# Eight dense tokens moved from the first expert pass to row gathers, in a one-core PEER layer

## The chip, the cores and the metric

The kernel runs on one core of one Trainium2 chip. The metric is the device time of one execution in microseconds. One execution was also profiled, and the rows below come from its trace. TensorE (PE) does the matmuls, VectorE (DVE), ScalarE (ACT) and GpSimd (POOL) the elementwise work, and SyncE (SP) issues most loads; indirect row gathers are issued by POOL.

## The reference, cut to what matters

One layer on 512 tokens of width 1024. A gated token mixer comes first, then PEER: each token picks, in each of 8 heads, 16 of 128 x 128 = 16384 single-neuron experts, so 128 experts a token.

```python
def peer(xn, w_q, sub_keys, u_tab, v_tab):
    ...
    s_top, i_top = lax.top_k(sc, PEER_TOPK)                    # two half-key scores per head
    ...
    best, pos = lax.top_k(cand..., PEER_TOPK)                  # 16 of 256 candidates
    idx = ...; g = softmax(best)
    ue = u_tab[ib]; act = gelu(einsum("phkd,pd->phk", ue, tb)) # first table: 128 rows a token
    ve = v_tab[ib]
    return einsum("phk,phkd->pd", gb * act, ve)                # second table: 128 rows a token
```

The output is RMSNorm(x + mixer + PEER), float32, 512 x 1024.

## The kernel before

Tokens lie in four tiles of 128. Tile 0 is served by **gathers**: for each of its 128 expert slots one indirect DMA brings 128 rows of 4 KB (one expert row for each token), first from `u_tab` (`ru`; a DVE multiply with the normed tokens `t0`, summed into a column of `d0`), later from `v_tab` (`rv`; DVE adds the row, times its weight, to `acc0`). That is 256 gathers.

Tiles 1 to 3, 384 tokens (`TD`), are **dense**: they go against both whole tables, 128 blocks of 128 experts each. A block of the first table is 24 matmuls into `ph` (8 slices of the width, 3 products each of a high and a low part), with 128 expert columns as weights and 384 token columns moving; ACT takes the gelu (`hg`). 62 of these blocks are done early, as filling between other work, and 56 of those results are put into DRAM (`hd`) and read back (`hr`). The other 66 are done in the last loop. A block of the second table is 18 matmuls into `acc` (6 for each token tile), with 128 tokens of `wh`/`wl` as weights and 512 columns of the table moving.

The stages in order: input projections and mixer (to 345 us), output projection and second norm (`turn`, L332 to L341), the query stage (16 steps: projection `pq`, scores `pc`, top-16 on DVE), the gate stage, and the last loop (L838). In the gate stage three rounds of 8 steps turn indices and gates into dense gate tiles: each step makes two `one_hot` groups of 8 tokens on DVE, 32 short matmuls into `pg` and copies to `stg`; between the rounds `stg` is written to DRAM (`gd`) while 7 more `ph` blocks run. Every third step issues a gather. In the last loop, iteration i loads a `v_tab` block, splits it into `hi` and `lo` (ACT, DVE), makes `wf`, `wh`, `wl` from gates and `hg`, runs the 18 matmuls, then one `ph` block while there is one, then releases `pace[i]` gathers: ACT copies the indices (`eix`), POOL issues, DVE consumes; up to `GLEFT` gathers stay unconsumed in program order. `pace` shares the gathers out by weights: 2 while `ph` blocks remain (66 iterations), `GTAIL` in the next 58, 0 in the last 4. The rows of gathers lie in two rings used in turn, of `GR` = 3 and `DR` buffers. `hi`/`lo` have 3 buffers, shared by both tables; `raw` has 7.

The query stage and the gate stage keep the written order on each engine; elsewhere a scheduler may move instructions.

Of the kernel before, what the change touches and what calls it, by code (L numbers as in the profile page):

```python
# [8 lines left out]
F32 = mybir.dt.float32  # L9
# [8 lines left out]
P = 128  # L18
# [9 lines left out]
TG = TD - P  # L28
EPS = 1e-6
# [21 lines left out]
DR = 5  # L51
GTAIL = 0.5
LATE = 3
FP = (1, 2)
GLEFT = 5
GR = 3
TWO = ("xa", "xc", "cv", "hh", "yb", "gga", "sma")
# [3 lines left out]
def tile_block(ctx: ExitStack, tc: tile.TileContext, x, w_in, vecs, w_ax, w_out, n2row, w_q, skT,  # L61
# [21 lines left out]
    x2d = dram.tile([NTT, P, D], F32, name="x2d")  # L83

# [70 lines left out]
    with ExitStack() as fctx:  # L155
# [193 lines left out]
    d0 = gp.tile([P, P], F32, name="d0")  # L349

# [6 lines left out]
    def gather(tab, n, name):  # L357
        ix = gidx.get(name, ei0[:, n:n + 1])
# [35 lines left out]
    def h_mm(i, hi, lo):  # L394
        pt = ps_a(f"ph{i}")
        mm3(pt[:, :TD], lambda k: hi[:, k * P:(k + 1) * P], lambda k: lo[:, k * P:(k + 1) * P],
            lambda k: a1h[:, k, P:], lambda k: a1l[:, k, P:], range(KD))
        return pt

    def h_act(i, pt):  # L400
        g = ha.tile([P, TD], F32, tag="hg", name=f"hg{i}", bufs=AHEAD)
        act.activation(g, pt[:, :TD], AF.Gelu_apprx_tanh)
        if i >= NKEY - SPILL:
            act.dma_start(hd[i - (NKEY - SPILL)], g)
        else:
            hg[i] = g

    def h_get(i):
        if i not in hg:
            hg[i] = ha.tile([P, TD], F32, tag="hg", name=f"hr{i}", bufs=AHEAD)  # L410
            sync.dma_start(hg[i], hd[i - (NKEY - SPILL)])
        return hg[i]

    hd = dram.tile([max(SPILL, 1), P, TD], F32, name="hd")
# [43 lines left out]
    with ExitStack() as qctx:  # L458
# [197 lines left out]
    def gather_release(n, i):  # L656
        names, p = [], gpos[0]
        while len(names) < n and p < len(gsched):
            f, a = gsched[p]
            if f is not gather_w:  # L660
                names.append(("ru" if f is gather_u else "rv") + str(a))
            p += 1
        if names:
            t = dp.tile([P, 4], I32, tag="eix", name=f"eix{i}", bufs=4)
            for m, nm in enumerate(names):
                c = int(nm[2:])
                tc.keep_in_program_order(act.activation(t[:, m:m + 1], eall[:, 0, c:c + 1], AF.Copy))  # L667
# [13 lines left out]
    with ExitStack() as gctx:  # L681
# [22 lines left out]
        dve.scalar_tensor_tensor(g12[:, :, 1, :], by_sub(ptg), GSC, g12[:, :, 0, :], op0=ALU.mult, op1=ALU.subtract)  # L704

# [44 lines left out]
        NSUB = NDT * P // OC  # L750
        ohs = {u: one_hot(u) for u in range(OB)}
        h_turn(HPRO2, dve)
        for t_ in range(NDT):
            stg = sp.tile([P, P, P], F32, tag="stg", name=f"stg{t_}", bufs=1)
            for s2 in range(P // OC // 2):
                sub = t_ * (P // OC) + 2 * s2

                def mid():
                    for u in (sub, sub + 1):
                        gate_mm(u, *ohs.pop(u))  # L760
# [8 lines left out]
                gather_steps(GSTEP[(sub // 2) % len(GSTEP)], 2)  # L769
# [21 lines left out]
    gdone = sum(1 for f, _ in gsched[:gpos[0]] if f is not gather_w)  # L791
    ng = 2 * P - gdone
# [41 lines left out]

    late = []
    vr = {}
    fgb = None
    for i in range(NKEY):  # L838
# [4 lines left out]
        wf = dp.tile([P, TD], F32, tag="wf", name=f"wf{i}", bufs=2)  # L843
# [4 lines left out]
        dve.tensor_tensor(wf[:, TG:], stg[:, i, :], hv_[:, TG:], op=ALU.mult)  # L848
# [71 lines left out]
```

## Time and profile before

| | |
|---|---|
| median of 3 runs | 1619.81 us (1617.53 to 1622.06) |
| the profiled execution | 1617.53 us, of which the span in the trace is 1615.4 us |
| PE busy, weight load busy | 1595.6 us (99%), 1412.5 us (87%) |
| DVE, ACT, POOL busy | 1264.4 us (78%), 688.2 us (43%), 510.8 us (32%) |
| granted TensorE clock, mean | 0.999 of full speed |
| bytes moved | 379.09 MB, 235 GB/s over the span |

Busy times are unions over the span. A matmul's duration in the trace holds its fill and drain, so that matmuls in a row overlap, and the time that one costs is the distance from start to start.

### The profile page before, as it was taken

The page shows a single profiled execution, that of the slowest core. Times are in us where ns is not written, and L with a number is a line of the kernel's source. Part 1 is how long each engine was busy: PE and PEld are TensorE (multiplying, and loading weights), DVE is VectorE, ACT ScalarE, POOL GpSimd, SP SyncE. Part 2 cuts the span into 40 slices and gives each one's busy share as a digit, 9 for nine tenths or more (in the row PEclk, how much of TensorE's full clock was granted, in tenths as well). Part 3 has the DMA queues.
Part 4 walks back from the last instruction along what each step waited for, and adds up shares of the span by engine and source line. Part 5 has one row for each costly group of instructions (what it writes and reads, how often), then busy time and mean ns, then how long its engine had stood idle before and what let it go on. Part 6 is the DMA issues. An engine that isn't in the chain of part 4 may idle for free.

```text
span 1615.4 us, 23573 instructions
## 1 busy us (share of the span) xinstructions
PE 1595.6 (99%) x8402; PEld 1412.5 (87%) x8402; DVE 1264.4 (78%) x2404; ACT 688.2 (43%) x1222; POOL 510.8 (32%) x379
## 2 busy tenths in 40 slices
PE   9999999999999999999999999999999999999997
PEld 8888888888988999999999888989998988887886
DVE  6666666645999997676878888888888789877767
ACT  7444444434333454454533433344333343333334
POOL 0000000004787840000045554545444554223231
PEclk9999999999999999999999999999999999999999
DMA  6222222334333356969499999999999999998884
GB/s 243 95 95 95 95 95 95 91 112 175 107 124 112 126 180 189 304 214 301 153 317 328 344 324 331 342 328 332 340 335 336 323 334 362 340 320 288 305 305 153
DMA packets 158453, 379.09 MB, mean 235 GB/s; under 512 B 14080, under 2 KB 78592, under 8 KB 158208
## 3 DMA queue, kind: packets, MB, share of 16 engines
q1 hardware_dynamic: 112832, 230.25, 41.6%
q0 software_dynamic: 36864, 134.23, 23.5%
q10 hardware_dynamic: 8640, 13.11, 2.3%
q8 instruction: 65, 1.06, 0.3%
q14 instruction: 52, 0.43, 0.1%
HBM read 345.56 MB, written 31.98 MB: 234 GB/s over the span
## 4 chain that ended last, share of the span: by engine, by line
PE 70%; DVE 9%; DMA 8%; issue 7%; POOL 3%; ACT 1%; SPq 1%; DVEq 0%; POOLq 0%; ACTq 0%
PE ph L147 7%; PE ph L149 7%; PE ph L148 7%; PE acc L830 7%; PE acc L833 6%; PE acc L829 6%; PE pin L149 6%; PE pin L147 6%; PE pin L148 6%; DMA ru<-in_u_tab_dram,eix 4%; DMA rv<-in_v_tab_dram,eix 3%; POOL rv L362 2%; PE pq L147 2%; PE pq L149 2%; PE pq L148 2%
## 5 line engine op out<-in xcount | busy, mean ns | idle before, releaser
L147 PE MATMUL ph<-a1h,hi_u 128*128 128x384 f32 x1024 | 346.3, 338 | 0.0
L149 PE MATMUL ph<-a1h,lo_u 128*128 128x384 f32 x1024 | 343.6, 336 | 0.6 <-POOL lo_u L108 0.4
L148 PE MATMUL ph<-a1l,hi_u 128*128 128x384 f32 x1024 | 342.7, 335 | 0.0
L830 PE MATMUL acc<-lo_v,wh 128*128 128x512 f32 x768 | 301.0, 392 | 5.1 <-DVE lo_v L108 5.1
L829 PE MATMUL acc<-hi_v,wh 128*128 128x512 f32 x768 | 299.5, 390 | 0.0
L362 POOL DMA_INDIRECT rv<-in_v_tab_dram,eix x128 | 168.1, 1313 | 265.0 <-ACT eix L667 229.7
L833 PE MATMUL acc<-hi_v,wl 128*128 128x512 f32 x768 | 238.7, 390 | 0.0
L362 POOL DMA_INDIRECT ru<-in_u_tab_dram,eix x120 | 161.0, 1341 | 216.7 <-ACT eix L667 178.3
L385 DVE SCALAR_TENSOR_TENSOR acc<-rv,w,acc 128x1024 f32<-128x1024 f32 x128 | 164.4, 1285 | 75.8 <-DMA rv<-in_v_tab_dram,eix 75.4
L107 ACT ACTIVATE hi_v<-raw_v 128x1024 fp32r<-128x1024 f32 x128 | 135.0, 1055 | 182.8 <-PE ph L148 169.3
L371 DVE SCALAR_TENSOR_TENSOR ru<-ru,t 128x1024 f32<-128x1024 f32 x128 | 155.7, 1222 | 57.0 <-DMA ru<-in_u_tab_dram,eix 56.9
L148 PEld LDWEIGHTS ph<-a1l,hi_u 128*128 128x128 f32 x1024 | 192.3, 188 | 2.6
L147 PEld LDWEIGHTS ph<-a1h,hi_u 128*128 128x128 f32 x1024 | 192.3, 188 | 2.6
L149 PEld LDWEIGHTS ph<-a1h,lo_u 128*128 128x128 f32 x1024 | 192.1, 188 | 1.5 <-POOL lo_u L108 0.8
L849 ACT ACTIVATE wh<-wf 128x384 fp32r<-128x384 f32 x128 | 67.0, 524 | 268.9 <-PE acc L830 193.0
L830 PEld LDWEIGHTS acc<-lo_v,wh 128*128 128x128 f32 x768 | 144.2, 188 | 38.9 <-DVE lo_v L108 10.1
L149 PE MATMUL pin<-a1h,lo_in 128*128 128x512 f32 x448 | 174.4, 389 | 0.3 <-POOL lo_in L108 0.3
L148 PE MATMUL pin<-a1l,hi_in 128*128 128x512 f32 x448 | 174.4, 389 | 0.0
L147 PE MATMUL pin<-a1h,hi_in 128*128 128x512 f32 x448 | 174.3, 389 | 0.0
L833 PEld LDWEIGHTS acc<-hi_v,wl 128*128 128x128 f32 x768 | 144.1, 188 | 30.7
L829 PEld LDWEIGHTS acc<-hi_v,wh 128*128 128x128 f32 x768 | 144.1, 188 | 27.4 <-ACT hi_v L107 0.2
L108 DVE TENSOR_TENSOR lo_v<-raw_v,hi_v 128x1024 fp32r<-128x1024 f32 x128 | 155.9, 1218 | 3.4 <-ACT hi_v L107 3.4
(199 smaller groups left out, 2469.9 us busy)
## 6 DMA issues: line engine op xcount, KB each, us to landing
raw_u<-in_uT_dram SPq DMA_DIRECT2D x128, 512.0 KB, 5.4
raw_v<-in_v_tab_dram SPq DMA_DIRECT2D x128, 512.0 KB, 5.6
raw_in<-in_w_in_dram SPq DMA_DIRECT2D x56, 512.0 KB, 3.3
gd<-stg SPq DMA_DIRECT2D x8, 2048.0 KB, 17.8
gt<-gd SPq DMA_DIRECT2D x128, 128.0 KB, 5.0
hd<-hg ACTq DMA_DIRECT2D x56, 192.0 KB, 3.4
hr<-hd SPq DMA_DIRECT2D x56, 192.0 KB, 5.5
raw_q<-in_w_q_dram SPq DMA_DIRECT2D x16, 512.0 KB, 3.2
```

Of the source, the lines that this page charges most:

```text
L107: act.activation(hi, raw, AF.Copy)
L108: lo_eng.tensor_tensor(lo, raw, hi, op=ALU.subtract)
L147: pe.matmul(pt, wh(k), xh(k), start=start and m == 0, stop=False)
L148: pe.matmul(pt, wh(k), xl(k), start=False, stop=False)
L149: pe.matmul(pt, wl(k), xh(k), start=False, stop=stop and m == n - 1)
L362: ins = pool.indirect_dma_start(out=rows, out_offset=None, in_=tab, in_offset=bass.IndirectOffsetOnAxis(ap=ix, axis=0))
L371: dq.append(lambda: dve.scalar_tensor_tensor(rows, rows, 1.0, t0, op0=ALU.mult, op1=ALU.mult, accum_out=d0[:, n:n + 1]))
L385: dq.append(lambda: dve.scalar_tensor_tensor(acc0, rows, w0[:, n:n + 1], acc0, op0=ALU.mult, op1=ALU.add))
L829: pe.matmul(accs[t][h], wh[:, ts], hi[:, hsl], start=first, stop=False)
L830: pe.matmul(accs[t][h], wh[:, ts], lo[:, hsl], start=False, stop=False)
L833: pe.matmul(accs[t][h], wl[:, ts], hi[:, hsl], start=False, stop=last)
L849: act.activation(wh, wf, AF.Copy)
```

## The change

The last eight tokens of tile 3 (`TE` = 8) leave the first pass: `ph` and `hg` become 376 columns wide (`TDE`), and the gate stage makes 47 groups of eight tokens instead of 48. These eight tokens have 8 x 128 = 1024 expert rows in each table. They are gathered with 16 partitions to a token, so that 8 gathers of 128 rows bring the `u_tab` rows (`xxu`) and 8 the `v_tab` rows (`xxv`). For this the normed rows `tx` are made on POOL, written to DRAM and read back with each row on 16 partitions (`te`); indices and gates take the same way (`ee`, `eg`). DVE sums the weighted `v_tab` rows in `acce`, and in iteration 48 (`XADD`) a one-hot matmul adds the 16 partitions of each token into `acc` of tile 3. The second pass keeps its width: the eight columns of `wf` are zero. `DR` goes from 5 to 4, `GLEFT` from 5 to 4, `GTAIL` from 0.5 to 0.7, and the gate stage issues no gather in its first two steps.

```diff
+TE = 8
+TDE = TD - TE
-DR = 5
-GTAIL = 0.5
+DR = 4
+GTAIL = 0.7
-GLEFT = 5
+GLEFT = 4
+XADD = 48
...
+        tx = fp.tile([P, D], F32, tag="junk", name="tx", bufs=1)
+        pool.tensor_scalar(tx, xs[NTT - 1], r, None, op0=ALU.mult)
+        pool.tensor_tensor(tx, tx, n2b, op=ALU.mult)
         turn_out(pts, 12, a1h, a1l)
...
+        act.dma_start(txd, tx[P - TE:, :])
...
+    def gather_xu(n):
+        rows = gather(u_tab, n, f"xxu{n}")
+        dq.append(lambda: dve.scalar_tensor_tensor(rows, rows, 1.0, te, op0=ALU.mult, op1=ALU.mult,
+                                                   accum_out=de[:, n:n + 1]))
+
+    def gather_xw(_):
+        act.activation(de, de, AF.Gelu_apprx_tanh)
+        dve.tensor_tensor(de, de, eg, op=ALU.mult)
+
+    def gather_xv(n):
+        rows = gather(v_tab, n, f"xxv{n}")
+        def add():
+            if n == 0:
+                acce.append(gp.tile([P, D], F32, tag="te", name="acce", bufs=1))
+                dve.tensor_scalar(acce[0], rows, de[:, 0:1], None, op0=ALU.mult)
+            else:
+                dve.scalar_tensor_tensor(acce[0], rows, de[:, n:n + 1], acce[0], op0=ALU.mult, op1=ALU.add)
+        dq.append(add)
...
-        mm3(pt[:, :TD], lambda k: hi[:, k * P:(k + 1) * P], lambda k: lo[:, k * P:(k + 1) * P],
-            lambda k: a1h[:, k, P:], lambda k: a1l[:, k, P:], range(KD))
+        mm3(pt[:, :TDE], lambda k: hi[:, k * P:(k + 1) * P], lambda k: lo[:, k * P:(k + 1) * P],
+            lambda k: a1h[:, k, P:P + TDE], lambda k: a1l[:, k, P:P + TDE], range(KD))
...
+            if s_ == 8:
+                for e in range(TE):
+                    sync.dma_start(te[e * EK:(e + 1) * EK, :], txd[e:e + 1, :].partition_broadcast(EK))
...
-    gsched = []
+    gsched = [(gather_xu, n) for n in range(TE)]
     for h in range(HEADS):
         for n in range(h * TOPK, (h + 1) * TOPK):
             gsched.append((gather_u, n))
+        if h == 0:
+            gsched.append((gather_xw, 0))
+            gsched.extend((gather_xv, n) for n in range(TE))
...
+        last = (NTT - 1, slice(P - TE, P))
+        act.dma_start(eed, eall[last[1], last[0], :])
+        act.dma_start(egd, gall[last[1], last[0], :])
+        for e_, d_ in ((ee, eed), (eg, egd)):
+            pool.dma_start(e_, d_.rearrange("e (k n) -> (e k) n", n=TE))
...
-        NSUB = NDT * P // OC
+        NSUB = TDE // OC
...
-                gather_steps(GSTEP[(sub // 2) % len(GSTEP)], 2)
+                if sub // 2 == 1:
+                    act.activation(eei, ee, AF.Copy)
+                if sub // 2 > 1:
+                    gather_steps(GSTEP[(sub // 2) % len(GSTEP)], 2)
...
+    wfs = [dp.tile([P, TD], F32, name=f"wf{m}") for m in range(2)]
+    for wf in wfs:
+        dve.memset(wf[:, TDE:], 0.0)
...
-        dve.tensor_tensor(wf[:, TG:], stg[:, i, :], hv_[:, TG:], op=ALU.mult)
+        dve.tensor_tensor(wf[:, TG:TDE], stg[:, i, :P - TE], hv_[:, TG:], op=ALU.mult)
...
+        if i == XADD:
+            bf = dp.tile([P, TG], F32, tag="gt", name="bf", bufs=4)
+            br = strm.tile([P, TD], F32R, tag="wh", name="br", bufs=3)
+            dve.memset(bf[:, :P], 0.0)
+            dve.tensor_reduce(bf[:, P - TE:P], ident.rearrange("p (e k) -> p e k", k=EK), op=ALU.add, axis=AX.X)
+            act.activation(br[:, :P], bf[:, :P], AF.Copy, scale=GSC)
+            hi, lo = split(acce[0], "acce", dve)
+            for part in (hi, lo):
+                for h in range(2):
+                    pe.matmul(accs[NDT - 1][h], br[:, :P], part[:, h * 512:(h + 1) * 512], start=False, stop=False)
```

## Rows read from the trace of the kernel before

**Rows 1.** The page: busy time by engine; shares of the chain that ended last.

```profile
PE 1595.6 (99%) x8402; PEld 1412.5 (87%) x8402; DVE 1264.4 (78%) x2404; ACT 688.2 (43%) x1222; POOL 510.8 (32%) x379
...
PE 70%; DVE 9%; DMA 8%; issue 7%; POOL 3%; ACT 1%; SPq 1%; DVEq 0%; POOLq 0%; ACTq 0%
```

**Rows 2.** Windows: stretch and length; busy time (instructions) by engine; clock, DMA share, GB/s.

```profile
395.00:515.00 120.00, 120.00 (x631) 107.44 (x630) 115.84 (x625) 41.00 (x75) 94.97 (x75) 1.00 0.36 121
515.00:565.00 50.00, 50.00 (x281) 47.90 (x280) 49.52 (x255) 18.23 (x38) 41.04 (x28) 1.00 0.35 120
565.00:665.00 100.00, 98.75 (x760) 96.81 (x759) 78.20 (x66) 47.89 (x76) 20.67 (x10) 1.00 0.66 207
...
740.00:795.00 55.00, 52.72 (x470) 50.93 (x469) 50.16 (x50) 29.45 (x51) 1.68 (x1) 1.00 0.60 205
795.00:1353.00 558.00, 554.32 (x2794) 502.12 (x2793) 465.67 (x649) 217.78 (x481) 263.25 (x201) 1.00 0.93 329
1353.00:1594.00 241.00, 239.81 (x1054) 197.23 (x1053) 189.93 (x307) 92.79 (x167) 65.83 (x47) 1.00 0.89 312
```

**Rows 3.** Windows of tile ph alone: PE busy, weight loads busy, ACT busy.

```profile
395.00:515.00 120.00, 45.63 (x249) 42.76 (x250) 4.92 (x10) 1.00 0.36 121
...
565.00:665.00 100.00, 83.17 (x466) 79.88 (x465) 9.78 (x20) 1.00 0.66 207
...
795.00:1353.00 558.00, 289.66 (x1598) 280.01 (x1596) 31.69 (x67) 1.00 0.93 329
```

**Rows 4.** Timeline of PE, first and last of 18 matmuls 384 wide (start, duration).

```profile
902.02 0.33 PE L147 MATMUL ph<-a1h,hi_u 128*128 128x384 f32 x1
...
904.97 0.33 PE L149 MATMUL ph<-a1h,lo_u 128*128 128x384 f32 x1
```

**Rows 5.** Timeline of PE, first and last of 19 matmuls 512 wide.

```profile
99.76 0.39 PE L149 MATMUL pin<-a1h,lo_in 128*128 128x512 f32 x1
...
103.84 0.39 PE L149 MATMUL pin<-a1h,lo_in 128*128 128x512 f32 x1
```

**Rows 6.** Timeline of PE: eight matmuls 128 wide with four-byte weights, and the next.

```profile
393.44 1.06 PE L515 MATMUL pc<-sks,qs 128*128 128x128 f32 x8
394.25 0.48 PE L147 MATMUL pq<-a1h,hi_q 128*128 128x512 f32 x1
```

**Rows 7.** Chain that ended last, gate stage: start, length, what.

```profile
729.01 19.74 DMA gd<-stg
...
785.42 1.15 DVE oij L714
786.59 1.24 DVE o L716
```

**Rows 8.** Timeline of POOL where the query stage begins.

```profile
382.55 0.18 POOL L461 IOTA ic<- 128x50 f16 x1 [366.75 <-PE pt_n L133]
382.71 2.41 POOL L108 TENSOR_TENSOR lo_q<-raw_q,hi_q 128x1024 fp32r<-128x1024 f32 x1
```

**Rows 9.** Groups by line: gathers and their consumers (busy, mean ns; idle before).

```profile
L362 POOL DMA_INDIRECT rv<-in_v_tab_dram,eix x128 | 168.1, 1313 | 265.0 <-ACT eix L667 229.7 <-issue 15.5 <-DVE acc L385 7.2
L385 DVE SCALAR_TENSOR_TENSOR acc<-rv,w,acc 128x1024 f32<-128x1024 f32 x128 | 164.4, 1285 | 75.8 <-DMA rv<-in_v_tab_dram,eix 75.4
...
L371 DVE SCALAR_TENSOR_TENSOR ru<-ru,t 128x1024 f32<-128x1024 f32 x128 | 155.7, 1222 | 57.0 <-DMA ru<-in_u_tab_dram,eix 56.9
```

**Rows 10.** Waits: who waited for whom, us in total, times, longest.

```profile
DVE acc L385 <- DMA rv<-in_v_tab_dram,eix: 75.4, 44, 5.0
...
ACT stg L729 <- DMA gd<-stg: 6.7, 1, 6.7
...
PE acc L830 <- DVE lo_v L108: 5.1, 9, 1.0
```

**Rows 11.** DMA issues: queue, count, size, median us to landing.

```profile
raw_v<-in_v_tab_dram SPq DMA_DIRECT2D x128, 512.0 KB, 5.6
raw_in<-in_w_in_dram SPq DMA_DIRECT2D x56, 512.0 KB, 3.3
```

More of the change, by code (lines that the diff above doesn't have):

```diff
@@ L83, in tile_block @@
     x2d = dram.tile([NTT, P, D], F32, name="x2d")
+    txd = dram.tile([TE, D], F32, name="txd")
+    eed = dram.tile([TE, P], F32, name="eed")
+    egd = dram.tile([TE, P], F32, name="egd")
+    EK = P // TE
     @contextmanager
@@ L349, in tile_block @@
     d0 = gp.tile([P, P], F32, name="d0")
+    ee = gp.tile([P, TE], F32, name="ee")
+    eg = gp.tile([P, TE], F32, name="eg")
+    eei = gp.tile([P, TE], I32, name="eei")
+    de = gp.tile([P, TE], F32, name="de")
+    te = gp.tile([P, D], F32, tag="te", name="te", bufs=1)
     ha = ctx.enter_context(tc.tile_pool(name="ha", bufs=1))
@@ L357, in gather @@
     def gather(tab, n, name):
-        ix = gidx.get(name, ei0[:, n:n + 1])
+        ix = gidx[name] if name in gidx else (eei if name[1] == "x" else ei0)[:, n:n + 1]
         rp, nb = rpool[gcnt[0] % len(rpool)]
@@ L372, in gather_u @@
                                                    accum_out=d0[:, n:n + 1]))
+    def gather_xu(n):
[5 more added lines that the diff above has]
+        dve.tensor_tensor(de, de, eg, op=ALU.mult)
+    acce = []
+    def gather_xv(n):
[7 more added lines that the diff above has]
+        dq.append(add)
     def drain(left):
@@ L395, in h_mm @@
         pt = ps_a(f"ph{i}")
-        mm3(pt[:, :TD], lambda k: hi[:, k * P:(k + 1) * P], lambda k: lo[:, k * P:(k + 1) * P],
-            lambda k: a1h[:, k, P:], lambda k: a1l[:, k, P:], range(KD))
+        mm3(pt[:, :TDE], lambda k: hi[:, k * P:(k + 1) * P], lambda k: lo[:, k * P:(k + 1) * P],
+            lambda k: a1h[:, k, P:P + TDE], lambda k: a1l[:, k, P:P + TDE], range(KD))
         return pt
     def h_act(i, pt):
-        g = ha.tile([P, TD], F32, tag="hg", name=f"hg{i}", bufs=AHEAD)
-        act.activation(g, pt[:, :TD], AF.Gelu_apprx_tanh)
+        g = ha.tile([P, TDE], F32, tag="hg", name=f"hg{i}", bufs=AHEAD)
+        act.activation(g, pt[:, :TDE], AF.Gelu_apprx_tanh)
         if i >= NKEY - SPILL:
@@ L409, in h_get @@
         if i not in hg:
-            hg[i] = ha.tile([P, TD], F32, tag="hg", name=f"hr{i}", bufs=AHEAD)
+            hg[i] = ha.tile([P, TDE], F32, tag="hg", name=f"hr{i}", bufs=AHEAD)
             sync.dma_start(hg[i], hd[i - (NKEY - SPILL)])
         return hg[i]
-    hd = dram.tile([max(SPILL, 1), P, TD], F32, name="hd")
+    hd = dram.tile([max(SPILL, 1), P, TDE], F32, name="hd")
     hord = list(range(NKEY - SPILL, NKEY)) + list(range(NKEY - SPILL))
@@ L659, in gather_release @@
             f, a = gsched[p]
-            if f is not gather_w:
-                names.append(("ru" if f is gather_u else "rv") + str(a))
+            if f not in (gather_w, gather_xw):
+                names.append({gather_u: "ru", gather_v: "rv", gather_xu: "xxu", gather_xv: "xxv"}[f] + str(a))
             p += 1
@@ L665, in gather_release @@
             for m, nm in enumerate(names):
-                c = int(nm[2:])
-                tc.keep_in_program_order(act.activation(t[:, m:m + 1], eall[:, 0, c:c + 1], AF.Copy))
+                c = int(nm.lstrip("rxuv"))
+                e = ee[:, c:c + 1] if nm[0] == "x" else eall[:, 0, c:c + 1]
+                tc.keep_in_program_order(act.activation(t[:, m:m + 1], e, AF.Copy))
                 gidx[nm] = t[:, m:m + 1]
@@ L675, in gather_steps @@
             gpos[0] += 1
-            if f is not gather_w:
+            if f not in (gather_w, gather_xw):
                 n -= 1
@@ L759, in mid @@
                     for u in (sub, sub + 1):
-                        gate_mm(u, *ohs.pop(u))
+                        if u < NSUB:
+                            gate_mm(u, *ohs.pop(u))
                     for u in (sub + OB, sub + OB + 1):
@@ L790, in tile_block @@
     accs = [[ps_b(f"acc{t}_{h}") for h in range(2)] for t in range(NDT)]
-    gdone = sum(1 for f, _ in gsched[:gpos[0]] if f is not gather_w)
-    ng = 2 * P - gdone
+    gdone = sum(1 for f, _ in gsched[:gpos[0]] if f not in (gather_w, gather_xw))
+    ng = 2 * (P + TE) - gdone
     wts = [2 if i < NKEY - nlag else GTAIL if i < NKEY - 4 else 0 for i in range(NKEY)]
@@ L842, in tile_block @@
         sync.dma_start(gt, gd[i])
-        wf = dp.tile([P, TD], F32, tag="wf", name=f"wf{i}", bufs=2)
+        wf = wfs[i % 2]
         wh = strm.tile([P, TD], F32R, tag="wh", name=f"wh{i}", bufs=3)
```

## The prediction

> **What bounds the kernel now.** First the page: PE is busy 99% of the span and holds 70% of the chain that ended last [rows 1]. That says where to look, not what a shorter matmul gives: for that each stage has to be read. So I took busy times by stage [rows 2] and, in the same stretches, the share of tile `ph`, the only tile whose matmuls get shorter [rows 3]. In the query stage PE is full (120.0 of 120), but DVE has 115.8 of 120 and then 49.5 of 50: PE bounds the first 120 us, DVE the next 50. From 565 to 665 PE is full again. The last gate round (740 to 795) is DVE's: 50.2 of 55, and the chain runs through `one_hot` there without a gap to the end of the round [rows 7]; the round before looks the same. The last loop is PE's: 554.3 of 558 and 239.8 of 241, with DVE at 83% and 79%. But the DMA engines are nearly as full there: share 0.93 at 329 GB/s, then 0.89 at 312 GB/s [rows 2]. And 132 us of DVE's idle time there is waiting for gathered rows [rows 9, 10]. So in the last loop PE sets the time with a second limit close behind.
>
> **What a `ph` matmul gives.** Durations overlap, so I take starts. 384 columns: 17 steps in 904.97 - 902.02 = 2.95 us, 0.1735 us each [rows 4]. 512 columns: 18 steps in 4.08 us, 0.2267 us [rows 5]. 128 columns differ by 0.0532 us, 0.416 ns a column. Eight columns are 3.33 ns, a block of 24 matmuls 0.080 us, all 3072 matmuls 10.2 us if every one lay on the path. This needs the pace to be set by columns, not by the weight loads, whose busy time in `ph` (280 of 290 us) is close to PE's [rows 3]. The eight score matmuls with four-byte weights, a new load for each, take 0.81 us from the first start to the next group's, 0.10 us each [rows 6]; so loads can follow at 0.10 us, and 0.170 lies above that.
>
> The Trainium skill ("TensorE: Matmul & The Clock Gate", "Back-to-back issue gap") says that in a stream of load and matmul pairs the two together set the spacing, about 81 ns at 128 columns and 131 ns at 512. As an estimate from these figures a column is 0.13 ns, and all 3072 matmuls give 3.2 us, not 10.2. The trace differs (0.2267 us at 512), and the measured spacing decides.
>
> **The change part by part.**
>
> Query stage: 249 `ph` matmuls while PE leads [rows 3] x 3.33 ns = 0.8 us. From 515 on DVE leads, and a shorter matmul gives nothing.
>
> Gate stage: 466 matmuls from 565 to 665 [rows 3] give 1.6 us. The `ph` blocks between rounds two and three run under the `gd` write, whose landing (19.7 us) is on the chain and holds ACT's first copies for 6.7 us [rows 7, 10]: nothing there. In the last round group 47 goes, so DVE makes one pair less, 1.15 + 1.24 = 2.4 us [rows 7], at the end of a round where DVE is the chain. Its 16 short matmuls and two copies were beside that. One gather fewer is issued in the stage; its consumer falls out of the first round, where DVE has 22 us free in 100 [rows 2]: nothing. Gate stage together: -4.0 us; between -1.6 (PE is the next limit at once) and -4.9.
>
> Last loop, PE: 1598 matmuls [rows 3] x 3.33 ns = -5.3 us. The one-hot sum adds 4 matmuls of 0.2267 us, +0.9. Its split, reduce and copies (two 1.2 us DVE instructions by [rows 9], one ACT pass, one turn of `hi`/`lo`) happen once beside 8 us of matmuls: nothing; without cover 2.5 us. `acce` is complete some ten iterations in, long before iteration 48. The shorter `hg`, `wf` and `hd` are not on the path.
>
> Head of the query stage: two new POOL passes over 128x1024. The nearest row is POOL's subtract of that size, 2.41 us [rows 8]. POOL was idle for 366.75 us until 382.55, and the norm factor is ready somewhat before that, since the transposes use it. Both hidden: 0; both late: +4.8, with `lo_q` and then PE's second projection behind them. That projection starts one projection (24 x 0.2267 = 5.4 us) after the first, so most is covered: I take +0.5. Behind them ACT's `txd` write could hold the `a1h` copies; it lies in the same bound.
>
> New small DMAs: eight broadcasts on SP in step 8. Even at the 3.3 us of a quiet load each [rows 11] they hold SP 26 us, and the query loads behind them are issued three steps of 10.5 us ahead (5.4 for `pq`, 0.8 for `pc`, 4.2 for `ph`): 0. Indices and gates go out by ACT and back by POOL, two landings; ACT's `eei` copy waits for them two steps later, with `hi_u`, `hg` and `stg` queued behind it, and PE behind those. Two landings at 5.6 us [rows 11] are 11 us against two steps of about 7 us plus two `ph` blocks: 0, at worst +3.
>
> Gathers: 256 become 272. The gate stage issues 7 instead of 8, leaving 265 instead of 248 for the last loop. Weights before: 66 x 2 + 58 x 0.5 = 161, so 203 gathers in the first 66 iterations and 45 in the next 58. After: 172.6, so 203 and 62. The denser part keeps its rate (3.07 an iteration), and all 17 more go to the tail, 0.77 to 1.07 an iteration. POOL: 17 x 1.3 us over a POOL 27% busy: 0. DVE: 17 x 1.2 = 20 us on 190 of 241 [rows 2, 9], 89% of a slightly shorter tail: fits. DMA: an iteration of the tail has 512 KB of table, 128 of gates, 188 of `hr` and 1.07 x 512 of gathers, 1378 KB; 58 of them are 81.8 MB in 58 x 18 x 0.2267 = 236.7 us, 346 GB/s against 312 before.
>
> The Trainium skill ("DMA: Bandwidth & Descriptors", "Issuing engines are not separate DMA queues") says that transfers issued by SP, ACT and POOL run on the same 16 engines and interleave. The trace agrees: a 512 KB load lands in 3.3 us early and in 5.6 us beside the gathers [rows 11]. If the engines were already the bound, 17 x 0.524 MB at 329 GB/s would be an added 27 us.
>
> They are not the bound yet, since PE is full. What the fuller engines and the shorter `GLEFT` cost I bound from PE's idle time in the last loop: 3.7 + 1.2 = 4.9 us today [rows 2], while DVE waits for gathers 132 us [rows 9]; the waits are mostly absorbed by the three `hi`/`lo` buffers. Below: 0, or a small gain where an earlier consumer frees DVE. Above: PE idle up to four times as long, +15. I take +2, half as much waiting again, since the rate in the dense part is unchanged. `DR` from 5 to 4 costs 0: with the rings used in turn, the ring of 3 limits first.
>
> **Sum.** -0.8 - 4.0 - 5.3 + 0.9 + 0.5 = -8.7, and +2 gives -6.7 us. The profiled execution took 1617.5 us, 2.1 of them outside its span; from it 1610.8. It is the fastest of the three runs; the median is 2.3 above. Moved by the same difference the median is 1613.1; I say 1613. A time measured here tells 0.3%, 4.9 us, from no change; so the sum is only just a gain.
>
> **The rivals.**
>
> *The gain is eaten by gather waits.* Shorter PE iterations and equal gathers leave DVE less slack; `GLEFT` 4 puts each consumer one gather earlier. For it: DVE's long waits and the 5.1 us in which PE waits for `lo_v` [rows 10]. Against it: those 5 us are all that 132 us of waiting cost. With 4 to 13 us more of PE idle the net is -4.9 to +4.9: about 1618.
>
> *The tail becomes DMA-bound.* It needs 346 GB/s; the tail has shown 312, the dense part 329 [rows 2]. At 312 its 81.8 MB take 262 us, +25.6, net +17, 1637. At 329: 248.6 us, +12, net +3. It turns the sign past the bound below 327 GB/s. Against it: neither figure is a ceiling, since PE was full and asked for no more. This is the slower case.
>
> *The pace does not follow the columns* (weight loads hold it). Then the 7.7 us of shorter matmuls fall away, leaving the pair of one-hots, the one-hot sum, the head and the waits: -2.4 + 0.9 + 0.5 + 2 = +1, about 1621. Rows 4 to 6 speak against it.
>
> **Chances.** Forecast 0.50 (its own range 1608 to 1615); eaten gain 0.30; DMA-bound tail 0.14; pace not by columns 0.06. So faster 0.50, same 0.36, slower 0.14. The range 1607 to 1623 leaves out most of the DMA-bound tail and a gain beyond 12 us.
>
> **What would show it.** In the profile after: `ph` spaced 0.170 us; the gate stage some 4 us shorter; iterations with `ph` 0.08 us shorter; tail iterations still 4.08 us at about 346 GB/s. PE idle in the last loop well over 7 us would mean the first rival, tail iterations above 4.3 us the second. A late `a1h` or `lo_q` near 380 us, or ACT idle before `eei`, would break the zeros taken there.

## The result: slower by 0.67%

| | before | after |
|---|---|---|
| median, 13 runs each | 1619.81 us | 1629.9 us |
| ratio | | 1.0067, 95% interval 1.0054 to 1.0079 |
| profiled execution, its span | 1617.5, 1615.4 us | 1629.66, 1627.9 us |

The ratio is +10.9 us (8.7 to 12.8) where -6.7 was forecast; 1629.9 lies above the range's 1623. Below, every ratio is turned to microseconds by 1619.81.

Three points of each trace divide the loss: the first `acc` matmul, the last `ph` matmul and the last `acc` matmul.

| start of, us | before | after | part before | part after |
|---|---|---|---|---|
| first `acc` | 797.17 | 794.37 | | |
| last `ph` | 1351.09 | 1349.18 | 553.92 | 554.81 |
| last `acc` | 1607.35 | 1618.43 | 256.26 | 269.25 |

What precedes the last loop became 2.8 us shorter, the loop's dense part did not become shorter at all, and the stretch behind the last `ph` grew by 13.0. Behind the last `acc` another 1.4 us were lost. The windows of after, with the columns of [rows 2]:

```profile
565.00:665.00 100.00, 98.43 (x759) 96.55 (x758) 77.36 (x64) 49.75 (x81) 20.55 (x11) 1.00 0.69 220
...
740.00:795.00 55.00, 54.17 (x469) 52.58 (x469) 51.08 (x58) 29.83 (x52) 1.69 (x1) 1.00 0.58 201
795.00:1353.00 558.00, 554.38 (x2791) 500.42 (x2790) 464.85 (x652) 217.38 (x480) 274.41 (x202) 1.00 0.92 328
1353.00:1594.00 241.00, 236.15 (x1030) 192.23 (x1028) 201.00 (x311) 88.84 (x174) 111.97 (x64) 1.00 0.96 343
```

In the last line the GB/s are 343, close to the 346 worked out, but PE is idle 4.9 us where it was 1.2, and POOL's 64 instructions hold it 1.75 us each where 47 took 1.40 [rows 2].

The timeline of PE in after, first and last of 18 `ph` matmuls:

```profile
899.06 0.34 PE L155 MATMUL ph<-a1h,hi_u 128*128 128x376 f32 x1
...
902.01 0.33 PE L157 MATMUL ph<-a1h,lo_u 128*128 128x376 f32 x1
```

17 steps in 2.95 us are 0.1735 us each, to the digit the pace of 384 columns [rows 4]. The eight columns are gone and the time, in this block, is not. Over all 1518 steps inside the 66 blocks of the last loop the mean is 173.5 ns where it was 174.9: 2.1 us in all, where 3.33 ns a step would be 5.1.

The waits of after, which answer to [rows 10]:

```profile
DVE acc L426 <- DMA rv<-in_v_tab_dram,eix: 60.8, 41, 4.2
DVE ru L388 <- DMA ru<-in_u_tab_dram,eix: 56.6, 45, 3.2
...
PE acc L887 <- DVE lo_v L116: 9.8, 12, 2.1
```

DVE's total waiting for rows did not grow, but PE's waiting for DVE did, and the timeline shows how. DVE in after:

```profile
1514.74 0.28 DVE L909 TENSOR_TENSOR wf<-stg,hr 128x120 f32<-128x120 f32 x1
1518.13 1.29 DVE L426 SCALAR_TENSOR_TENSOR acc<-rv,w,acc 128x1024 f32<-128x1024 f32 x1 [3.12 <-DMA rv<-in_v_tab_dram,eix]
1519.33 0.55 DVE L911 TENSOR_TENSOR wl<-wf,wh 128x384 fp32r<-128x384 f32 x1
1519.80 1.22 DVE L116 TENSOR_TENSOR lo_v<-raw_v,hi_v 128x1024 fp32r<-128x1024 f32 x1
```

and PE in after:

```profile
1520.04 0.39 PE L886 MATMUL acc<-hi_v,wh 128*128 128x512 f32 x1
1521.08 0.50 PE L887 MATMUL acc<-lo_v,wh 128*128 128x512 f32 x1 [0.65 <-DVE lo_v L116]
```

DVE stands 3.12 us before a row that hasn't landed; `wl` and the split `lo_v` stand behind it in DVE's order; PE gets to the matmul on `lo_v` as the split ends. The same is seen at 1538.19 (0.49). Then, near the end, PE's timeline in after has two longer stops:

```profile
1602.55 0.50 PE L887 MATMUL acc<-lo_v,wh 128*128 128x512 f32 x1 [1.78 <-DVE lo_v L116]
...
1604.79 1.22 PE L886 MATMUL acc<-hi_v,wh 128*128 128x512 f32 x2 [1.27 <-ACT hi_v L115]
1605.81 0.63 PE L887 MATMUL acc<-lo_v,wh 128*128 128x512 f32 x1
...
1610.93 0.41 PE L890 MATMUL acc<-hi_v,wl 128*128 128x512 f32 x1
```

The 12 steps from 1605.81 to 1610.93 take 0.427 us each instead of 0.227: 2.4 us more.

Where the 13.0 us lie is best counted in steps from start to start, since PE counts as busy while a matmul is stretched (0.63 us at the end where others have 0.39). The stretch behind the last `ph` is 62 iterations of 18 matmuls. What its steps take beyond 0.227 us adds up to 2.9 us in before and 15.9 in after; in the last six iterations alone it is 0.8 and 8.7. So 7.9 of the 13.0 us lie at the end, the two stops and the slower steps among them, and 5.1 in the 56 iterations ahead of it.

### The profile page after: what moved, and what is told of

Same layout as the page of the kernel before. It is cut to its first block, busy times and chain, and to the rows that moved or that the text cites. A ratio compares the mean times of both kernels' runs of the same rounds, so it can differ in the third digit from the quotient of the medians.

```text
span 1627.9 us, 23657 instructions
## 1 busy us (share of the span) xinstructions
PE 1600.8 (98%) x8390; PEld 1411.4 (87%) x8390; DVE 1282.2 (79%) x2432; ACT 689.9 (42%) x1241; POOL 572.6 (35%) x399
## 5 line engine op out<-in xcount | busy, mean ns | idle before, releaser
L155 PE MATMUL ph<-a1h,hi_u 128*128 128x376 f32 x1024 | 345.8, 338 | 0.0
L157 PE MATMUL ph<-a1h,lo_u 128*128 128x376 f32 x1024 | 343.4, 335 | 0.7 <-POOL lo_u L116 0.7
L156 PE MATMUL ph<-a1l,hi_u 128*128 128x376 f32 x1024 | 343.0, 335 | 0.0
L379 POOL DMA_INDIRECT rv<-in_v_tab_dram,eix x128 | 196.7, 1537 | 195.2 <-ACT eix L715 165.6
L379 POOL DMA_INDIRECT ru<-in_u_tab_dram,eix x128 | 178.1, 1391 | 189.6 <-ACT eix L715 161.2
## 6 DMA issues: line engine op xcount, KB each, us to landing
gd<-stg SPq DMA_DIRECT2D x8, 2048.0 KB, 14.9
```

The costliest lines, as they stand in the source:

```text
L155: pe.matmul(pt, wh(k), xh(k), start=start and m == 0, stop=False)
L156: pe.matmul(pt, wh(k), xl(k), start=False, stop=False)
L157: pe.matmul(pt, wl(k), xh(k), start=False, stop=stop and m == n - 1)
```

## The experiments

Two theories stood against each other. **Pace and rows:** the 376-wide matmuls run no faster than 384-wide ones, and the added gathers land too late for DVE. **Rivals:** the pace is held by weight loads; or one of the small edits (`GLEFT`, the last iterations) or the DMA rate itself is the price.

| run | against before (95%) | us |
|---|---|---|
| the change | 1.0067 (1.0054 to 1.0079) | +10.9 |
| e2_wide: `ph` 384 again | 1.0086 (1.0065 to 1.0107) | +13.9 |
| e13_368: `ph` 368 | 1.0007 (0.9991 to 1.0023) | +1.1 |
| e16_shift: `a1h`, `a1l` 16 bytes on | 1.0109 (1.009 to 1.0127) | +17.7 |
| e17_shift5: the same, `GTAIL` 0.5 | 1.0041 (1.0017 to 1.0064) | +6.6 |
| e18_start4: `ph` reads 4 columns on | 1.0016 (0.9999 to 1.0033) | +2.6 |
| e3_nogather: no added gathers | 0.999 (0.9978 to 1.0002) | -1.6 |
| e7_gtail: the change, `GTAIL` 0.5 | 1.0023 (1.0004 to 1.0042) | +3.7 |
| e10_gtail_only: before, `GTAIL` 0.7 | 1.0055 (1.0034 to 1.0076) | +8.9 |
| e6_tail: before, `GTAIL` 0.7, `GLEFT` 4, `DR` 4 | 1.0034 (1.0015 to 1.0054) | +5.5 |
| e14_gtail3: before, `GTAIL` 0.3 | 1.0 (0.9989 to 1.001) | 0 |
| e4_gleft: the change, `GLEFT` 5 | 1.0077 (1.0056 to 1.0099) | +12.5 |
| e5_early: the change, gathers end earlier | 1.0051 (1.0034 to 1.0068) | +8.3 |
| e12_end: before, gathers end earlier | 1.0001 (0.9985 to 1.0017) | +0.2 |
| e8_lean: the change, less other traffic | 0.9997 (0.9985 to 1.001) | -0.5 |
| e9_halfdve: the change, half of DVE's row work | 1.0 (0.9984 to 1.0015) | 0 |

### The pace of a matmul

**e1_width**, a kernel of matmuls alone, 48 for each width, all else left out (shortened):

```
WIDTHS = (512, 448, 416, 400, 392, 384, 376, 352, 320, 256)
...
for r in range(NREP):
    k = r % KD
    pe.matmul(pt[:, :n], w[:, k * P:(k + 1) * P], m[:, :n], start=r == 0, stop=r == NREP - 1)
dve.tensor_copy(res[:, :n], pt[:, :n])
```

> Only matmuls, 48 in a row for each width, each with a weight load of its own; the layer is left out. Theory 1 (weight loads hold the pace of a high/low-part matmul at about 0.173 us): 512, 448 and 416 columns follow the columns (0.227, 0.200, 0.187 us from start to start), 400 lies near 0.180, and 384, 376, 352, 320 and 256 all stand at 0.173. Rival (the pace follows the columns down to the loads of the score matmuls): 376 at 0.170, 320 at 0.147, 256 at 0.120. A third outcome, 376 alone slow and 352 or 320 fast, would mean that the odd width itself costs.

The timeline of DVE in it, the copies behind the groups of 392, 384, 376 and 352 columns:

```profile
64.46 0.57 DVE L85 COPY res<-fr 128x392 f32<-128x392 f32 x1 [7.93 <-PE fr L84]
72.78 0.56 DVE L85 COPY res<-fr 128x384 f32<-128x384 f32 x1 [7.75 <-PE fr L84]
81.09 0.55 DVE L85 COPY res<-fr 128x376 f32<-128x376 f32 x1 [7.76 <-PE fr L84]
88.83 0.52 DVE L85 COPY res<-fr 128x352 f32<-128x352 f32 x1 [7.18 <-PE fr L84]
```

The difference of two starts, divided by 48, is a group's pace: 384 columns 0.1733 us (8.32 / 48), 376 columns 0.1731 (8.31 / 48), 352 columns 0.1613. **e11_fine** took the widths between, `WIDTHS = (384, 380, 376, 372, ...)`:

> Only matmuls again, 48 in a row for each of ten widths between 336 and 384. In the first such run 384 and 376 took the same 0.173 us each, 352 took 0.161 and 320 took 0.147. If there is a step (a plateau under 384 that ends somewhere above 352), 380 and 372 stand at 0.173 too, and the first width below the plateau falls at once by over 0.005. If 376 alone is slow, 380, 372, 368 and 360 lie at 0.1717, 0.1683, 0.1667 and 0.1633, one column being 0.42 ns.

| columns | 400 | 392 | 384 | 380 | 376 | 372 | 368 | 352 | 320 | 256 |
|---|---|---|---|---|---|---|---|---|---|---|
| measured, ns | 180.2 | 177.3 | 173.3 | 171 | 173.1 | 170 | 166.9 | 161.3 | 146.7 | 119.8 |
| 0.416 ns a column from 384 | 180.0 | 176.6 | 173.3 | 171.6 | 170.0 | 168.3 | 166.6 | 160.0 | 146.7 | 120.0 |

Paces fall to 0.120 us, so weight loads don't hold them at 0.173: the rival of the weight loads is out. These widths follow the line within 2 ns but for 376, 3.1 ns above it (of the others tried, 378, 440 and 448 lie 2.5 to 3.4 ns above). **e15_376** asked which property of the 376-wide matmul it is (shortened, with comments added):

```
group("plain", 376)          # also 384, 378, 374, 368, 312, 440
group("shiftmoving", 376, off=4)   # m[:, 4:380]
group("shiftout", 376, po=4)       # pt[:, 4:380]
group("onetile", 376, one=True)    # the same weights each time
```

> Only matmuls, 48 in a row for each group, to see what makes 376 columns slow: 378 and 374 beside it; 376 with the moving columns starting 4 further on, with the output starting 4 further on, and with one and the same weight tile each time. By columns 376 is 0.170 us. If the width alone does it, all 376 groups stand at 0.173; if an alignment does, one of the shifted groups falls to 0.170; if the weight load does, the group with one weight tile. 374 and 378 near 0.169 and 0.171 would make it 376 alone; both above these by 0.002 or more, a region.

```profile
43.46 0.55 DVE L85 COPY res<-plain 128x376 f32<-128x376 f32 x1 [7.76 <-PE plain L83]
51.60 0.55 DVE L85 COPY res<-plain 128x374 f32<-128x374 f32 x1 [7.59 <-PE plain L83]
59.76 0.55 DVE L85 COPY res<-shiftmoving 128x376 f32<-128x376 f32 x1 [7.61 <-PE shiftmoving L83]
```

The lines are DVE's timeline again. 374 columns take 169.6 ns (8.14 / 48), and 376 columns that start four columns further on 170.0 (8.16 / 48): on the line. 376 stays at 173.1 with a moved output and at 173.3 with one weight tile. So for 376 it is the start of the moving operand together with this width; why, no run shows.

**In the kernel.** e2_wide undoes the narrowing alone:

```
-        mm3(pt[:, :TDE], lambda k: hi[:, k * P:(k + 1) * P], lambda k: lo[:, k * P:(k + 1) * P],
-            lambda k: a1h[:, k, P:P + TDE], lambda k: a1l[:, k, P:P + TDE], range(KD))
+        mm3(pt[:, :TD], lambda k: hi[:, k * P:(k + 1) * P], lambda k: lo[:, k * P:(k + 1) * P],
+            lambda k: a1h[:, k, P:P + TD], lambda k: a1l[:, k, P:P + TD], range(KD))
```

> The changed kernel with one thing undone: the first-table matmuls are 384 wide again (the last eight columns are computed and not read). Theory 1 (the narrower matmuls give nothing): the time of the changed kernel, 1630, within 2 us. Rival (they give their 10 us, and something else costs 20): 8 to 10 us slower, about 1639.

It is 3.0 us above the change, with about 4.0 either way: level with the first theory, and too wide to shut out a gain of some us. The paces above say it more sharply. e13_368 narrows further, to a width that is on the line (`TDH = TDE - 8` in `ph`, `hg`, `wf` and `hd`):

> The changed kernel with the first-table matmuls, their results and the weights made from them 368 wide (eight more tokens get no expert part); everything else, the 16 added gathers too, as in the change. A 368-column matmul was measured at 0.1667 us, against 0.1733 at 376 and 384. If PE's pace sets the time wherever I said so: 2305 matmuls on the path times 6.7 ns, 13 to 15 us faster than the changed kernel, about 1616. Rival (gathered rows and DVE set the last loop's time, so that a faster PE only waits more): less than 5 us faster, above 1625.

9.7 us under the change. 368 columns save 6.4 ns a matmul, 14.8 us over the 2313 matmuls of the forecast's three stages; two thirds came. In its trace 3.8 us are gained up to the first `acc` (790.58) and 3.4 in the dense part, none behind it. So a shorter `ph` does pay, if it is shorter. e16_shift moved the start of both operands for every reader:

```
-    a1h = const.tile([P, KD, S], F32R, name="a1h")
+    a1h = const.tile([P, KD * S + 8], F32R, name="a1h")[:, 4:4 + KD * S].rearrange("p (k s) -> p k s", k=KD)
```

(`a1l` likewise. Both tiles also grow by 32 bytes a partition, so that what lies behind them in SBUF may have moved too; e15_376 and e18_start4 are free of that.)

> The changed kernel with a1h and a1l begun 16 bytes later in SBUF, so that the 376 columns of every ph matmul start 4 elements further; nothing else is changed. If the start of the moving operand is what kept the 376-column matmuls at the time of 384, ph runs at 0.170 us a step here instead of 0.1735 in the trace of the change, and the last loop issues 1598 of them, the gate stage 466 and the query stage 249: 5.3 + 1.6 + 0.8 = 7.7 us if every one lay on the path; e13_368 gave back two thirds of what its matmuls saved, so about 5 us here, 1625 beside 1630, ratio 1.003 to 1.005. Rival: in the kernel something else sets the pace (loads and moving reads of both engines' other work), ph stays at 0.1735 and the ratio at 1.006 to 1.008.

It was slower, which neither theory expected. Its timeline of PE, first the projections of the first stage, 512 wide, then `ph`:

```profile
98.82 0.40 PE L155 MATMUL pin<-a1h,hi_in 128*128 128x512 f32 x1
...
104.42 0.40 PE L155 MATMUL pin<-a1h,hi_in 128*128 128x512 f32 x1
...
898.25 0.34 PE L155 MATMUL ph<-a1h,hi_u 128*128 128x376 f32 x1
...
901.17 0.33 PE L157 MATMUL ph<-a1h,lo_u 128*128 128x376 f32 x1
```

24 steps of 512 columns take 5.60 us, 0.2333 each against 0.2267 [rows 5], and the query stage's first matmul comes at 390.38 instead of 382.10; that alone is 8.3 us. `ph` runs at 0.1718 (2.92 / 17), half of what its expectation said, while the 512-wide `acc` matmuls, which do not read `a1h`, keep 0.227 in the median. The experiment mixed a loss with the gain. e18_start4 moves the start of `ph` alone:

```
-            lambda k: a1h[:, k, P:P + TDE], lambda k: a1l[:, k, P:P + TDE], range(KD))
+            lambda k: a1h[:, k, P + 4:P + 4 + TDE], lambda k: a1l[:, k, P + 4:P + 4 + TDE], range(KD))
```

> The changed kernel with the ph matmuls alone reading from column P + 4 to P + 380 in place of P to P + 376: the first expert pass takes tokens four later than it should, so the output is off, and nothing else moves. e16_shift moved all of a1h and thereby slowed the 512-wide projections of the first stage from 0.2267 to 0.2333 us a step, which hid what ph gives. Here those keep their start. If the start is what counts, ph runs at 0.170 to 0.172 us a step, the last loop's first part is 2.5 to 5.5 us shorter than the change's 554.8 us from the first acc matmul to the last of ph, and the total is 2 to 5 us under the change: ratio 1.003 to 1.0055 beside 1.0067. Rival: ph stays at 0.1735, ratio 1.006 to 1.008.

```profile
901.92 0.33 PE L155 MATMUL ph<-a1h,hi_u 128*128 128x376 f32 x1
...
906.00 0.39 PE L886 MATMUL acc<-hi_v,wh 128*128 128x512 f32 x1
```

24 steps in 4.08 us are 0.1700, the forecast's pace, and the time falls by 8.3 us (the interval of the difference is about 3.4 either way) where 3.33 ns on 2313 matmuls are 7.7. Its expectation had only 2 to 5 us; and its profiled execution, at 1628.75 the slowest of twelve, does not show the dense part shorter (790.49 to 1347.38). Up to the first `acc` 3.9 us are gained. In the dense part the `ph` steps inside blocks do take less, 258.6 us against 263.4, but PE's waits before `acc` matmuls there are 9.5 us against 3.4: in that execution the gain turned into waits. So by stage it is shown only ahead of the last loop.

### The price of the gathers

e3_nogather is the change without the sixteen added gathers and with the old weight:

```
-GTAIL = 0.7
+GTAIL = 0.5
...
-    gsched = [(gather_xu, n) for n in range(TE)]
+    gsched = []
...
-    ng = 2 * (P + TE) - gdone
+    ng = 2 * P - gdone
```

> The changed kernel without its 16 added gathers and their consumers (the last eight tokens get no expert part), and with the tail weight 0.5 of before, so that the tail has 45 gathers as before; narrow matmuls, GLEFT 4, DR 4, the small DMAs, the added POOL passes and the one-hot sum stay. Theory 2 (the added gathers in the tail are what costs): 1615 to 1619, at or a little under the kernel before, by the gate stage's 2.7 us less the sum's 0.9. Rival (GLEFT and DR make DVE late): 1625 to 1630. If the pace does follow the columns after all, 1609.

It is 12.5 us under the change: the gathers and where they are put cost that, and the rest of the change is worth -1.6 us. e6_tail puts the three numbers of the change into the kernel before, e10_gtail_only just the first of them, e7_gtail takes it back in the change, e14_gtail3 goes the other way:

```
-GTAIL = 0.5
+GTAIL = 0.7
```

> The kernel before with only its three constants changed as in the change: tail weight 0.7, GLEFT 4, DR 4. No gather is added, but 58 instead of 45 of the 248 lie in the tail (1.01 an iteration) and correspondingly fewer in the dense part. Theory 2 (the rate in the tail costs): slower by most of the 13 us that the changed kernel loses behind its last first-table block, 1626 to 1632. Rival (it is the number of gathers in all, or DVE's order): within 3 us of before.

> The changed kernel with the tail weight of before, 0.5: of its 265 gathers 48 lie in the tail instead of 62, and 217 instead of 203 in the dense part (3.3 an iteration). Theory 2 (the rate in the tail costs): most of the loss comes back, 1619 to 1623. Rival (the number of gathers costs, wherever they lie): 1628 to 1632, the stalls moving into the dense part.

> The kernel before with the tail weight 0.7 alone (GLEFT 5 and DR 5 stay). With all three constants it was 1.0034 of before. Theory 2 (the rate in the tail): the same 1.002 to 1.005. Rival (GLEFT and DR): 0.999 to 1.001.

> The kernel before with tail weight 0.3 instead of 0.5: 29 of 248 gathers in the tail, 0.5 an iteration, and 3.3 an iteration in the dense part instead of 3.1. If fewer gathers in the tail go on helping: 1614 to 1617, below both kernels. Rival (0.5 is where tail and dense part balance): 1619 to 1624.

With the same 256 gathers the weight 0.7 alone costs 8.9 us (5.5 to 12.3) in the kernel before, and 7.2 of the change's 10.9 go when it is taken back. By its trace e10_gtail_only has the dense part 4.2 us shorter (549.69) and the stretch behind it 14.9 longer (271.14). The sixteen gathers by themselves, at weight 0.5, are the distance from e3_nogather to e7_gtail: 5.3 us (about 3.6 either way). Below 0.5 nothing more is to be had. e4_gleft (`GLEFT` 5 in the change), e5_early and e12_end (`NKEY - 4` made `NKEY - 16` in the change and `NKEY - 8` in before) tried the rivals:

> The changed kernel with GLEFT 5 as before. Rival (each consumer stands one gather earlier on DVE, which is what makes DVE late): 1619 to 1624. Theory 2 (the rate in the tail): within 2 us of the changed kernel, 1628 to 1632.

> The changed kernel with no gathers released in its last 16 iterations instead of the last 4; the same gathers are shared out over the iterations before. Theory 3 (a good part of the loss is made at the end, where DVE has late gathers, the last table blocks and the first output tile to do at once, and TensorE then falls to the lower clock): 1622 to 1626, with no clock loss behind the last full iteration. Rival (the loss is spread over the tail by its rate): 1629 to 1634, since the rate before the end rises to about 1.25 an iteration.

> The kernel before with its last gather released eight iterations before the end instead of four, to try for a time below both. Theory 3 (gathers near the end make the last table blocks late and cost clock): 2 to 4 us faster than before. Rival (only moved forward): within 2 us.

`GLEFT` is not the cause: e4_gleft is not faster, and e6_tail, which has `DR` 4 and `GLEFT` 4 beside the weight, is not slower than e10_gtail_only. e12_end is level with before. e5_early is 2.6 us under the change, with about 3.4 either way, but it also moves gathers: by its weights 213 of the 265 now lie in the dense part, where the change has 203. Its trace shows that the end is dear and that the price moves. This is what the steps behind the last `ph` take beyond 0.227 us, one execution each:

| | before | after | e10_gtail_only | e5_early | e8_lean | e9_halfdve |
|---|---|---|---|---|---|---|
| first 56 iterations, us | 2.1 | 7.2 | 12.8 | 8.3 | -0.4 | 5.3 |
| last six, us | 0.8 | 8.7 | 5.1 | 0.3 | 6.5 | 2.0 |

In the other traces with weight 0.7 the last six iterations cost 6.4 to 8.4 us (e2, e4, e6, e13, e16, e18), in those with 0.5 or 0.3 only 0.3 to 2.8 (e3, e7, e12, e14), but for e17_shift5, profiled in the slowest of its executions, at 6.7. e5_early loses almost nothing at the end, but its dense part is 558.84 us, 4.0 longer than in after. So what the stops at the end cost is not settled by it.

Bytes or DVE? e8_lean leaves the gathers and takes other transfers out of the tail, e9_halfdve leaves the transfers and halves what DVE does with each row there:

```
e8_lean:
-        gt = dp.tile([P, TG], F32, tag="gt", name=f"gt{i}", bufs=4)
-        sync.dma_start(gt, gd[i])
+        if i < NKEY - nlag:
+            gt = dp.tile([P, TG], F32, tag="gt", name=f"gt{i}", bufs=4)
+            sync.dma_start(gt, gd[i])
...
+        if i >= NKEY - SPILL:
+            i = NKEY - SPILL - 1
         if i not in hg:
e9_halfdve:
+        wid[0] = D // 2 if i >= NKEY - nlag else D
...
-        dq.append(lambda: dve.scalar_tensor_tensor(acc0, rows, w0[:, n:n + 1], acc0, op0=ALU.mult, op1=ALU.add))
+        w = wid[0]
+        dq.append(lambda: dve.scalar_tensor_tensor(acc0[:, :w], rows[:, :w], w0[:, n:n + 1], acc0[:, :w], op0=ALU.mult, op1=ALU.add))
```

> The changed kernel with fewer other transfers in the tail: from iteration 66 on the gate tiles are not loaded, and from 72 on the first-pass results are not read back (tiles loaded earlier are used again, so the second pass computes with wrong weights there). That takes 316 of 1378 KB from a tail iteration, and the demand falls from 346 to about 267 GB/s; DVE's work and the gathers stay. Theory 2a (full DMA engines land the gathered rows late): 1617 to 1622, and gathers of the tail land sooner. Rival 2b (DVE's order and amount of work): within 3 us of the changed kernel, 1627 to 1633.

> The changed kernel with DVE consuming only half of each row gathered from iteration 66 on (the other half of those expert parts is left out), 0.65 us instead of 1.29 each; the transfers stay. Rival 2b (DVE has too much to do in the tail): 1617 to 1622. Theory 2a (late rows): DVE waits for the same landings, 1626 to 1631.

Either brings the time back to before, and by the table each takes away another part of the loss: e8_lean the stops in the first 56 iterations, e9_halfdve most of those at the end. The same window of the tail in before, after, e8_lean and e9_halfdve:

```profile
1353.00:1590.00 237.00, 235.81 (x1037) 193.89 (x1036) 186.10 (x299) 90.25 (x164) 65.83 (x47) 1.00 0.89 313
```

```profile
1353.00:1590.00 237.00, 232.15 (x1013) 189.23 (x1012) 198.01 (x307) 88.84 (x174) 111.97 (x64) 1.00 0.97 347
```

```profile
1353.00:1590.00 237.00, 237.00 (x1047) 196.33 (x1046) 206.03 (x319) 92.36 (x180) 92.70 (x65) 1.00 0.80 277
```

```profile
1353.00:1590.00 237.00, 233.08 (x1022) 191.10 (x1021) 174.24 (x312) 90.25 (x183) 78.98 (x65) 1.00 0.97 350
```

e9_halfdve moves 350 GB/s and is not slower than before, so the rate is no ceiling. e8_lean has DVE busy for 206.0 of 237 us and PE full, so DVE's work isn't one either. So it is the two together. DVE's waits for rows in this window, in before, after and e8_lean:

```profile
DVE acc L385 <- DMA rv<-in_v_tab_dram,eix: 44.4, 17, 5.0
DVE ru L371 <- DMA ru<-in_u_tab_dram,eix: 6.7, 7, 2.1
```

```profile
DVE acc L426 <- DMA rv<-in_v_tab_dram,eix: 27.2, 14, 3.7
DVE ru L388 <- DMA ru<-in_u_tab_dram,eix: 11.8, 8, 3.0
```

```profile
DVE acc L426 <- DMA rv<-in_v_tab_dram,eix: 21.2, 23, 3.2
DVE ru L388 <- DMA ru<-in_u_tab_dram,eix: 8.8, 9, 2.9
```

Busy time and these waits add up to 186.1 + 51.1 = 237.2 us in before, 198.0 + 39.0 = 237.0 in after and 206.0 + 30.0 = 236.0 in e8_lean. DVE waits for next to nothing but rows, in all three, and in e8_lean PE loses nothing by it: the sum does not tell a tail that loses from one that does not. How late the rows come and how fast DVE makes it up might. From the timeline of after, a DVE iteration with one row takes 3.32 us (`lo_v` at 1526.88 to `lo_v` at 1530.20), 1.20 of it the row: 2.12 without. As an estimate from that, DVE needs 3.04 of 4.08 us at 0.77 rows an iteration and 3.40 at 1.07: what it can make up after a late row falls from 1.04 to 0.68 us an iteration, 4.2 to 2.7 us in four. Stops of some 3 us come every four iterations in after (1518.13, 1535.24, 1553.50, 1570.35, 1586.69). Before has such stops too, and longer ones:

```profile
1484.76 1.29 DVE L385 SCALAR_TENSOR_TENSOR acc<-rv,w,acc 128x1024 f32<-128x1024 f32 x1 [4.97 <-DMA rv<-in_v_tab_dram,eix]
```

So it is not that the waits grew; less room to make them up is what fits. This last step is argued from rows; shown is that easing either side, the transfers or DVE's part, gives the time back. Whether rows land sooner in e8_lean cannot be read: its trace has no landings of gathers. The waits by releaser in this stretch show where DVE's lateness goes next, in before and then in after:

```profile
ACT wh L849 <- DVE wf L848: 47.8, 17, 4.4
```

```profile
ACT wh L910 <- DVE wf L909: 75.5, 28, 4.9
```

In e8_lean this wait is 20.9 us, in e9_halfdve 15.9.

**e17_shift5** joined `GTAIL` 0.5 to e16_shift:

> The same with GTAIL 0.5, as in the kernel before: the two terms that the runs found wrong are both mended. The change with GTAIL 0.5 alone stood at 1.0023. If the pace of ph gives 5 us here too, the ratio is about 0.999, between 0.997 and 1.001, so at best level with the kernel before. Rival: with the gathers' rows late in the dense part PE's shorter matmuls only wait longer, and the ratio stays at 1.001 to 1.004.

11.0 us under e16_shift, the tail's price a third time. It missed its expectation: it is 6.6 us above before, near the 8.3 that the 512-wide projections lost. e18_start4's start with `GTAIL` 0.5 was not run; as an estimate from these differences it would lie near before or a few us under it, which would also need other tokens chosen.

## Why the prediction missed

Two steps failed: the pace of the narrower matmul, and what the added gathers in the tail cost. With both put right the sum is -8.7 + 7.7 (the pace) + 12.5 (the gathers by e3_nogather, in place of the +2) = +11.5, and +10.9 was measured.

- **"128 columns differ by 0.0532 us, 0.416 ns a column. Eight columns are 3.33 ns"**: the slope holds from 512 down to 256 columns for most widths, but 376 from this start takes 173.1 ns where the line has 170.0, and 378, 440 and 448 are off it as well. Of the -0.8, -1.6 and -5.3 of `ph` next to nothing came: the dense part took 554.8 us after 553.9. The rival "the pace does not follow the columns" had a chance of 0.06; its effect came, but not its cause: rows 4 to 6 spoke against weight loads, and e1_width bears that out with 0.120 us at 256 columns. A slope between two widths need not hold at a third.
- **"I take +2, half as much waiting again"**, with "DVE: 17 x 1.2 = 20 us on 190 of 241, 89% ...: fits" behind it. The forecast read DVE's waits for rows as time to spare ("the waits are mostly absorbed by the three `hi`/`lo` buffers"). They were not once more rows came: e3_nogather puts the added gathers and their placing at 12.5 us, 7.2 of them the weight 0.7 (e7_gtail) and 5.3 the sixteen gathers. A busy share of 89% left out the order: `wl` and `lo_v` stand behind a late row on DVE, and PE behind them. That added rows took from what DVE makes up after a late one is argued above, not shown. The mechanism, PE held by gather waits, is that of the first rival, "the gain is eaten by gather waits"; its 4 to 13 us of PE idle hold the 12.5, and only with no gain to eat did it turn the sign. The forecast had no term for the clock, whose fall at the end cost 2.4 us in the profiled execution.
- **The second rival, a DMA-bound tail**, got its rate (347 GB/s against the 346 worked out) without its price: e9_halfdve runs at 350 in before's time. That its +12 at 329 GB/s lies beside the 12.5 is chance. The Trainium skill ("DMA: Bandwidth & Descriptors", "Issuing engines are not separate DMA queues") has the transfers of all issuing engines share 16 engines and interleave. In the tail the median row landed 8.0 us after its issue where it was 7.2, which would agree; but it is 7.2 in before's dense part too, at 329 GB/s, so that the sharing made the rows later is not shown.
- **Gate stage, -4.0**: -2.4 of it was group 47, and 2.8 us were found before the first `acc` matmul, which fits it, though no run has group 47 alone; the 1.6 of `ph` was not found.
- **Head, +0.5**: `lo_q` starts at 385.93 us instead of 382.71 [rows 8], inside the bound of 4.8; POOL waits 2.14 us more for the landing of `txd`, which the forecast had not counted on POOL. No loss is seen behind it: 2.8 us are gained up to the first `acc`, where group 47 was forecast at 2.4.
- **The zeros for the small DMAs, `DR` and `GLEFT`** held: no wait of PE behind `eei`, e4_gleft is not faster, and e6_tail is not slower than e10_gtail_only.
- **One-hot sum, +0.9**: not told apart in the runs; e3_nogather contains it and is at -1.6, where the forecast's other terms without `ph` and waits give -1.0.

## What to carry to other kernels

A change that narrows a matmul should first be run as that width at that start, by itself: 376 columns gave next to nothing where 368, or 376 starting 16 bytes on, followed the slope. On an engine that works in order, time spent waiting for late data is not time to spare: see what stands behind the wait, and who waits for that. Count a loss in steps from start to start as well as in idle time: PE's idle time grew by 3.7 us where its steps grew by 13.0. Where an edit adds work and also sets where it is put, price the placing by itself on the old kernel: one constant cost 8.9 us there.

## What the runs showed of the hardware

- The start of the moving operand matters to the matmul's pace in both directions: 16 bytes on, 376 columns go from 173.1 to 170.0 ns (e15_376), and the 512-wide projections that read `a1h` and `a1l` from 226.7 to 233.3 (e16_shift). The Trainium skill ("TensorE: Matmul & The Clock Gate", "Back-to-back issue gap") gives one spacing for a width; 376 columns at two starts had two.
- After the stops at the end (PE busy 4.14 us of the 8 before 1605) TensorE fell to the lower of its two levels, 1.2 GHz: granted clock 0.51 from 1605 to 1611, and matmuls 0.427 us apart. The windows of after around it, columns as in [rows 2]:

```profile
1597.00:1605.00 8.00, 4.14 (x13) 1.97 (x12) 6.58 (x14) 4.68 (x7) 0.00 (x0) 0.94 0.17 66
1605.00:1611.00 6.00, 6.00 (x15) 4.65 (x16) 2.37 (x3) 0.72 (x2) 0.00 (x0) 0.51 0.00 0
```

- A gather's instruction on POOL took 984 ns in the median for `rv` in before's tail and 1456 in after's, at DMA shares of 0.89 and 0.97. The share is not the reason by itself: in e9_halfdve, at 0.97 too, it took 1090. What makes it longer stays open.
